# One decoder layer in float32: the down-projection as seven block products with their sums held in PSUM, and banded attention scores on 128 rows

## The chip, the cores and the metric

The kernel runs on one core of a Trainium2 chip. The metric is device time in microseconds, from the first to the last instruction with what the launch adds around them; a lower time is better. TensorE (PE, with its weight loads PEld) multiplies, VectorE (DVE), ScalarE (ACT) and GpSimd (POOL) do elementwise work, and SyncE (SP) issues the DMAs.

## The reference, cut to what matters

One layer of a decoder over 1024 tokens of width 1024, all in float32: a token mixer (attention over a window of 128 and a gated linear recurrence), cross-attention to 256 memory tokens, and a gated MLP of width 2816 with a convolution over three positions.

```python
s = einsum('bnqhgd,bnkhd->bnhgqk', q, [k_prev, k_here]) * 64**-0.5   # blocks of 128, heads of 64
u = h @ w_up                            # [1024, 2816*2]
u = causal_depthwise_conv3(u) + conv_b
gate, val = split(u, 2)
y = (gelu_tanh(gate) * val) @ w_down    # [1024, 2816] @ [2816, 1024]
x = x + rms_norm(y, ffn_post_norm)
```

## The kernel before, in words

Every product is made of three matmuls, since each operand x is split into a rounded part hi and a rest lo (`split`: a cast on ACT at L73, a subtraction at L74 on DVE or POOL): hi·hi, hi·lo and lo·hi. [...] The program is written in Python loops over tiles of 128 tokens or 128 features; a scheduler puts the instructions of each engine into one fixed order and inserts the waits. Buffers come from pools: `up` (U, 44 tiles of 4 KB per partition), `hs` (HS, 3), `hh` (HH, 3), and in PSUM `pj` (PJ, two tiles of two banks) and `sm` (SM, four tiles of one bank). A new tile takes the place of an older one, and its first writer waits for the last user of that one, whichever engine or DMA that is. SP issues all DMAs, in order.

*Attention scores* (`swa`, a generator that is advanced by `tick` between other matmuls). A query tile `q[h]` holds, for head h, the hi part in the 64 partitions of that head and the lo part in the other 64; the key tile `kah[h]` holds the hi part of the keys in both halves. One matmul over 128 rows (L387) therefore gives hi·hi + lo·hi; a second one (L389) gives hi·lo over the 64 rows of the head alone, from one tile `kal` that holds both heads.

*Up-projection* (`Pair`, `prod`, L934). It is done as seven block products for each of 22 feature blocks j: 12 matmuls each, 84 per block. Their weight sums are made on DVE (`wprep`), and `up_load(j + 2)` loads the weights two blocks ahead. `gate` and `value` apply the convolution; `value` stores the 128x1024 result into `gd[j]` in DRAM.

*Down-projection* (`down`, `dn_prep`, L1122). The 22 row blocks of `w_dn` are taken in chunks of 2 and then five times 4. For each chunk, each of 8 token tiles and each half of 512 output columns, 3 matmuls per row block are summed in one SM tile, and DVE adds that into `yacc` (L1129). Per row block `gd[j]` and `w_dn` (512 KB each) are loaded and split. In the last chunk `finish` normalizes a tile, adds the residual `x2` and stores.

Of the kernel before, what the change touches and what calls it, by code (L numbers as in the profile page):

```python
# [18 lines left out]
P = 128  # L19
# [16 lines left out]
def tile_layer(ctx: ExitStack, tc: tile.TileContext, a: dict, out: bass.AP):  # L36
# [305 lines left out]
    swam = cpool.tile([P, 2 * P], F32, name="swam")  # L342
# [4 lines left out]
    late(dve.tensor_copy(lvm, lvf))  # L347
    AT = U("AT", (P, NB, P))
    late(pool.memset(AT, 0.0))
    Ad = cpool.tile([P, NB, 32], F32, name="Ad")  # L350
    late(pool.memset(Ad, 0.0))


    HEADS = (slice(0, 64), slice(64, P))

    def head_split(src, s):
        hi, lo = [U(s + "s", (P, 1024), F32R) for _ in range(2)], U(s + "l", (P, 1024), F32R)
        for h, r in enumerate(HEADS):
            act.copy(hi[h][r], src[r])
            dve.tensor_tensor(lo[r], src[r], hi[h][r].bitcast(F32), op=ALU.subtract)  # L360
        return hi, lo

    kah, kal = head_split(ka, "ka")
    for h, r in enumerate(HEADS):
        sp.dma_start(kah[h][HEADS[1 - h]].bitcast(F32), kah[h][r].bitcast(F32))

    def q_split(src):
        hi, lo = head_split(src, "qa")
# [6 lines left out]
    def swa(j, q):  # L375
        for g in range(2):
            s = [HS("s", (P, 2, 2, 2 * P)) for _ in range(2)]
            mx = ST("mx", 8)
            for i in range(2):
                pss = [SM("s", (P, 2, 2 * P)) for _ in range(2)]  # L380
                first = g == 0 and i == 0
                for b in range(2):
                    n = g * 4 + 2 * i + b
                    lo = P if n == 0 else 0
                    qc, kc = slice(n * P, (n + 1) * P), slice((n - 1) * P + lo, (n + 1) * P)
                    for h in range(2):
                        pe.matmul(pss[h][:, b, lo:], q[h][:, qc], kah[h][:, kc], start=True, stop=False)  # L387
                    for h, r in enumerate(HEADS):
# [433 lines left out]
    gd = dram.tile([NF, P, T], F32, name="gd")  # L822

    hR = []

# [133 lines left out]
    def value(u, j, g):  # L959
        c = HH("c")  # L960
        conv(u, NF + j, c)
        dve.tensor_tensor(c, g, c, op=ALU.mult)
        sp.dma_start(gd[j], c)

    class Pair:
        def __init__(self, j, x=None, z=None):
# [92 lines left out]
    up_load(3)  # L1059
    for j in range(2, NF):  # L1060
        prev, cur = cur, Pair(j)
        cur.q1()
        wprep(j, 3)
        wprep(j, 7)
        cur.q5()
        wprep(j + 1, 1)
        wprep(j, 4)
        up_load(j + 2)
        cur.q2()
        wprep(j + 1, 5)  # L1070
        wprep(j + 1, 2)
        cur.q6()
# [9 lines left out]
    w_fpost = bcast_row(a["ffn_post_norm"], "wfp", U)  # L1082
    chunks = [(0, 1)] + [tuple(range(c, c + 4)) for c in range(2, NF, 4)]
    dn = {}

    def dn_prep(j):
        g, w = HS("g"), HH("wd")
        sp.dma_start(w, w_dn[j * P:(j + 1) * P, :])
        sp.dma_start(g, gd[j])
        dn[j] = split_u(g, "g"), split_u(w, "wd")  # L1090

    yacc = [None] * NB

    def finish(tb, yw, ss, xt):
# [3 lines left out]
        for ch in range(2):  # L1098
            c = slice(ch * 512, (ch + 1) * 512)
# [3 lines left out]
    def down(n, js):  # L1103
        last, fin = n == len(chunks) - 1, None
        junk = U("junk") if last else None
        nxt = [] if last else list(chunks[n + 1])
        for tb in range(NB):
            if yacc[tb] is None:
                yacc[tb] = U("yacc")
            if last:  # L1110
                xt, yw, ss = HH("x2"), HS("yw"), ST("ss", 2)
                sp.dma_start(xt, x2d[tb])
            if tb % 2 == 1 and nxt:
                dn_prep(nxt.pop(0))
            for ch in range(2):
                c = slice(ch * 512, (ch + 1) * 512)
                ps = SM("dn")
                m = 0
                for j in js:
                    (ghi, glo), (whi, wlo) = dn[j]  # L1120
                    for l, r in ((ghi, whi), (ghi, wlo), (glo, whi)):
                        pe.matmul(ps, l[:, tb * P:(tb + 1) * P], r[:, c],  # L1122
                                  start=(m == 0), stop=(m == 3 * len(js) - 1))
                        m += 1
                y = yacc[tb][:, c]
                if n == 0:
                    act.copy(y, ps)
                else:
                    dve.tensor_tensor(y, ps, y, op=ALU.add)  # L1129
                if last:  # L1130
                    act.activation(junk[:, c], y, AF.Square, scale=1.0 / 32, accum_out=ss[:, ch:ch + 1])  # L1131
                    dve.tensor_tensor(yw[:, c], y, w_fpost[:, c], op=ALU.mult)
            if last:
                if fin is not None:
                    finish(*fin)
                fin = (tb, yw, ss, xt)
            yield
        if last:
            finish(*fin)
        for j in js:  # L1140
            dn[j] = None
# [58 lines left out]
```

## Time and profile before

| what | value |
|---|---|
| median of 3 runs | 1460.9 us (1457.65 to 1462.75) |
| the profiled execution, its time | 1458.89 us |
| its span, first to last instruction | 1457.1 us |
| granted clock of TensorE, mean | 0.996 |
| PE busy | 1428.9 us (98%) |
| DVE busy | 877.3 us (60%) |
| ACT busy | 623.5 us (43%) |
| POOL busy | 82.0 us (6%) |
| DMA | 130.69 MB, mean 90 GB/s |

Busy is the time in which an engine had an instruction in work. A matmul's stated length includes the time in which it overlaps its neighbours, so how fast matmuls follow each other is read from their starts. POOL issues no DMA in this kernel.

### The profile page before, as it was taken

How to read it: one execution, taken by the hardware profiler on the slowest of the kernel's cores; microseconds unless marked ns; L12 is line 12 of the kernel's file. 1: busy time of each engine (PE TensorE's matmuls, PEld its weight loads, DVE VectorE, ACT ScalarE, POOL GpSimd, SP SyncE). 2: the span in 40 equal slices, each digit the busy share in tenths (PEclk: the TensorE clock that was granted, in tenths of full speed). 3: DMA queues.
4: the chain of work that ended last, by engine and by line, in shares of the span. 5: the costliest groups of instructions: out<-in, count | busy, mean ns of one | idle time of the engine just before them, and what ended most of it. 6: DMA issues, size and time to landing. Idle time of an engine off the chain costs nothing.

```text
span 1457.1 us, 21512 instructions
## 1 busy us (share of the span) xinstructions
PE 1428.9 (98%) x8770; PEld 1183.8 (81%) x8770; DVE 877.3 (60%) x1263; ACT 623.5 (43%) x1156; POOL 82.0 (6%) x148
## 2 busy tenths in 40 slices
PE   7999999999999999999999999999999999999997
PEld 6978887777898888887888788888888877888886
DVE  4446616565675553457347997787777747444436
ACT  4453533526454433345335655555454537212102
POOL 3100100000010110011111000000000000000001
PEclk9999999999999999999999999999999999999999
DMA  7132102020853252013223332222222127333104
GB/s 225 37 94 45 30 8 52 16 60 20 213 152 106 91 174 58 1 44 130 87 87 101 84 104 87 70 76 87 88 87 82 48 72 270 120 116 116 59 29 159
DMA packets 121872, 130.69 MB, mean 90 GB/s; under 512 B 12789, under 2 KB 100270, under 8 KB 121774
## 3 DMA queue, kind: packets, MB, share of 16 engines
q1 hardware_dynamic: 121774, 129.32, 28.6%
q8 instruction: 69, 1.13, 0.3%
q14 instruction: 29, 0.24, 0.0%
HBM read 101.52 MB, written 25.17 MB: 87 GB/s over the span
## 4 chain that ended last, share of the span: by engine, by line
PE 91%; DVE 5%; ACT 2%; DMA 1%; issue 1%; POOL 0%; SPq 0%; DVEq 0%; POOLq 0%; ACTq 0%
PE xz L934 22%; PE dn L1122 16%; PE co L676 6%; PE po L676 6%; PE cq L236 5%; PE y L934 4%; PE pv L256 3%; PE pqa L236 3%; PE pm L649 3%; PE pf L236 3%; PE pg L236 3%; PE pq L236 3%; PE cq L227 2%; PE sc L764 1%; PE po L444 1%; PE lv L459 1%
## 5 line engine op out<-in xcount | busy, mean ns | idle before, releaser
L934 PE MATMUL xz<-th,w 128*128 128x512 f32 x960 | 306.5, 393 | 2.3 <-DVE ug L994 1.2
L934 PEld LDWEIGHTS xz<-th,w 128*128 128x128 f32 x960 | 180.2, 188 | 48.6 <-DVE ug L994 5.9
L934 PE MATMUL xz<-tl,w 128*128 128x512 f32 x480 | 187.1, 390 | 0.0
L1122 PE MATMUL dn<-wdl,gh 128*128 128x512 f32 x352 | 137.1, 389 | 0.1
L1122 PE MATMUL dn<-wdh,gh 128*128 128x512 f32 x352 | 136.2, 390 | 0.8 <-ACT wdh L73 0.8
L1122 PE MATMUL dn<-wdh,gl 128*128 128x512 f32 x352 | 137.0, 389 | 0.0
L1129 DVE TENSOR_TENSOR yacc<-dn,yacc 128x512 f32<-128x512 f32 x80 | 55.1, 690 | 96.5 <-PE dn L1122 95.8
L934 PEld LDWEIGHTS xz<-tl,w 128*128 128x128 f32 x480 | 90.2, 188 | 17.4
L74 DVE TENSOR_TENSOR wl<-w,wh 128x1024 fp32r<-128x1024 f32 x59 | 73.1, 1249 | 32.1 <-ACT wh L73 32.0
L73 ACT CAST w<-w 128x512 fp32r<-128x512 f32 x105 | 62.6, 621 | 43.8 <-PE xz L934 30.2
L74 DVE TENSOR_TENSOR w<-w,w 128x512 fp32r<-128x512 f32 x105 | 69.9, 688 | 18.2 <-ACT w L73 17.9
L1122 PEld LDWEIGHTS dn<-wdh,gh 128*128 128x128 f32 x352 | 66.0, 188 | 15.1 <-ACT wdh L73 1.2
L1122 PEld LDWEIGHTS dn<-wdl,gh 128*128 128x128 f32 x352 | 66.1, 188 | 14.3 <-DVE wdl L74 0.5
L1122 PEld LDWEIGHTS dn<-wdh,gl 128*128 128x128 f32 x352 | 66.1, 188 | 13.8
L73 ACT CAST wh<-w 128x1024 fp32r<-128x1024 f32 x64 | 66.0, 1056 | 10.4 <-DMA w<-in_ca_wq 5.1
L73 ACT CAST gh<-g 128x1024 fp32r<-128x1024 f32 x22 | 23.1, 1052 | 101.4 <-PE dn L1122 91.8
L934 PE MATMUL y<-th,w 128*128 128x512 f32 x168 | 55.2, 389 | 0.0
L883 DVE TENSOR_TENSOR s<-w 128x512 f32<-128x512 f32 x21 | 14.5, 691 | 50.8 <-PE xz L934 50.8
L1131 ACT ACTIVATE junk<-yacc 128x512 f32<-128x512 f32 x16 | 10.1, 633 | 73.4 <-DVE yacc L1129 73.4
L398 DVE SCALAR_TENSOR_TENSOR s<-s,swam 128x512 f32<-128x512 f32 (+2 forms) x40 | 20.7, 553 | 33.3 <-PE s L389 33.3
L676 PE MATMUL po<-wh,mh 128*128 128x512 f32 x128 | 40.0, 393 | 0.0
L676 PE MATMUL co<-VWh,pth 128*128 128x512 f32 x128 | 40.0, 393 | 0.0
(310 smaller groups left out, 3260.9 us busy)
## 6 DMA issues: line engine op xcount, KB each, us to landing
w<-in_ffn_w_up SPq DMA_DIRECT2D x44, 512.0 KB, 4.7
gd<-c SPq DMA_DIRECT2D x22, 512.0 KB, 2.6
g<-gd SPq DMA_DIRECT2D x22, 512.0 KB, 5.7
wd<-in_ffn_w_down SPq DMA_DIRECT2D x22, 512.0 KB, 3.4
x<-in_x SPq DMA_DIRECT2D x16, 512.0 KB, 3.1
w<-in_w_in SPq DMA_DIRECT2D x16, 512.0 KB, 7.2
w<-in_ca_wk SPq DMA_DIRECT2D x8, 512.0 KB, 5.7
w<-in_ca_wv SPq DMA_DIRECT2D x8, 512.0 KB, 5.5
```

The lines of the kernel that those rows point to most:

```text
L73: act.copy(hi, src)
L74: eng.tensor_tensor(lo, src, hi.bitcast(F32), op=ALU.subtract)
L227: pe.matmul(ps[:, t0:t0 + n], l[:, k, :], r[:, k % 2, c:c + n], start=(m == 0), stop=(m == 23))
L236: pe.matmul(ps[:, half * 512:(half + 1) * 512], l[:, k, :], hts[half][k // 2][sel][:, k % 2, :], start=(k == 0 and j == 0), stop=(k == KD ...
L256: pe.matmul(ps[:, tb % 4, :], l[:, k % 2, c:c + P], r[:, k % 4, :], start=(m == 0), stop=(m == 23))
L398: dve.scalar_tensor_tensor(s[i][:, b0:b1, h, lo:], pss[h][:, b0:b1, lo:], 0.125, swam[:, lo:].rearrange("p (a k) -> p a k", a=1) .to_broad ...
L444: pe.matmul(po[r, b, :], va[:, n - 1 + kb, r], ptt[:, h, kb, :], start=(kb == kbs[0]), stop=(kb == 1))
L649: pe.matmul(ps[:, i, :], l[:, k, :], r[:, k % 4, :], start=(n == 0), stop=(n == 23))
L676: pe.matmul(ps[:, ch * 512:(ch + 1) * 512], l, r[:, ch * 512:(ch + 1) * 512], start=(k == 0 and j == 0), stop=(k == KD - 1 and j == 2))
L934: pe.matmul(ps, l[k], r[k // 2][:, k % 2, :], start=start and m == 0, stop=stop and m == last, skip_group_check=True)
L1122: pe.matmul(ps, l[:, tb * P:(tb + 1) * P], r[:, c], start=(m == 0), stop=(m == 3 * len(js) - 1))
L1129: dve.tensor_tensor(y, ps, y, op=ALU.add)
```

## The change

Three parts. **Down-projection:** tokens, features and output columns are each cut in two, and the product of 2x2 blocks is made of seven block products (`PASSES`, the numbers of the up-projection's products). One pass goes over 11 pairs of row blocks (m) and four token tiles (b): 12 matmuls per step, 77 steps. Its four results stay in PSUM from pass to pass (`bank_a` in the four SM tiles, `bank_b` in the two PJ tiles) and are drained after a pass. The left operands (tokens by features) are summed on DVE in `rows_out`, after `value`, and stored as eight half-size pieces of `gd`. The right operands (sums of blocks of `w_dn`) are made by DMAs that POOL issues (`dn_sums`): into a tile `ws` with plain and adding DMAs, and from there into `wsd` in DRAM. Each step loads two pieces of 256 KB (`dn_load`), ahead by 5 to 16 steps, and splits them (`dn_ahead`). **Scores:** the keys' lo part gets a tile per head that holds it in both halves, so the second matmul runs over 128 rows as well (and adds lo·lo). **Buffers:** `hh` has 4 tiles; `swam` and `Ad` move into one of them.

```diff
-    hh = ctx.enter_context(tc.tile_pool(name="hh", bufs=3))
+    hh = ctx.enter_context(tc.tile_pool(name="hh", bufs=4))
...
+    kal = [U("kal", (P, 1024), F32R) for _ in range(2)]
+    kah = head_split(ka, "ka", kal)
+    for t in (kah, kal):
+        for h, r in enumerate(HEADS):
+            sp.dma_start(t[h][HEADS[1 - h]].bitcast(F32), t[h][r].bitcast(F32))
...
                         pe.matmul(pss[h][:, b, lo:], q[h][:, qc], kah[h][:, kc], start=True, stop=False)
-                    for h, r in enumerate(HEADS):
-                        pe.matmul(pss[h][:, b, lo:], q[h][r, qc], kal[r, kc], start=False, stop=True)
+                        pe.matmul(pss[h][:, b, lo:], q[h][:, qc], kal[h][:, kc], start=False, stop=True)
...
-        sp.dma_start(gd[j], c)
+        rows_out(j, c)
+    def rows_out(j, c):
+        m = j // 2
+        if j % 2 == 0:
+            t = U("gt", (P, 2, 512))
+            dve.tensor_tensor(t[:, 0], c[:, :512], c[:, 512:], op=ALU.subtract)
+            sp.dma_start(gd[1, m], c[:, :512])
+            sp.dma_start(gd[5, m], t[:, 0])
+            held[m] = c, t
+        else:
+            c0, t = held.pop(m)
+            t4 = U("gt", (P, 512))
+            dve.scalar_tensor_tensor(t[:, 1], t[:, 0], -1.0, c[:, 512:], op0=ALU.mult, op1=ALU.subtract)
+            dve.tensor_tensor(c0[:, 512:], c[:, 512:], c0[:, 512:], op=ALU.subtract)
+            dve.scalar_tensor_tensor(t4, t[:, 1], -1.0, c[:, :512], op0=ALU.mult, op1=ALU.subtract)
...
+    def dn_sums(m):
+        t = U("ws", (P, 2, 512))
+        pool.dma_start(t[:, 0], dn_src(0, 1, m))
+        pool.dma_start(t[:, 1], dn_src(0, 0, m))
+        pool.dma_start(t[:, 0], dn_src(1, 1, m), accum_op=ALU.add)
+        pool.dma_start(t[:, 1], dn_src(0, 1, m), accum_op=ALU.add)
+        pool.dma_start(wsd[5, m], t[:, 0])
+        pool.dma_start(wsd[7, m], t[:, 1])
+        pool.dma_start(t[:, 0], dn_src(0, 0, m), accum_op=ALU.add)
+        pool.dma_start(wsd[6, m], t[:, 0])
+        pool.dma_start(t[:, 0], dn_src(1, 0, m), accum_op=ALU.add)
+        pool.dma_start(wsd[3, m], t[:, 0])
+    PASSES = (1, 5, 6, 3, 7, 2, 4)
+    steps = [(n, m) for n in PASSES for m in range(NM2)]
...
+    def dn_mm(ps, i, b, start, stop):
+        hi, lo = dn_op[i]
+        c = slice(b * P, b * P + P)
+        for k, (l, r) in enumerate(((hi, hi), (hi, lo), (lo, hi))):
+            pe.matmul(ps, l[:, 0, c], r[:, 1, :], start=start and k == 0, stop=stop and k == 2,
+                      skip_group_check=True)
...
+            for m in range(NM2):
+                i = p * NM2 + m
+                more = max(0, min(11, (i - 3 * NM2) // 2))
+                dn_ahead(i, *((7, 4) if p == 0 else (5 + more, 2 + more)))
+                for b in range(4):
+                    dn_mm(bank[b], i, b, n in (1, 5, 2) and m == 0, m == NM2 - 1)
...
     cur.q3()
-    next(first)
+    go(1)
     cur.q7()
     g = gate(cur.ug, NF - 1)
-    next(first)
+    go(2)
     cur.q4()
```

On PE the scores of one block pair of the first head pair (`s` the PSUM tiles, `kas` and `kal` the keys, `qas` the queries) stand before as follows.

```order
L387 MATMUL s_805<-kas_692,qas_758 128x256
L387 MATMUL s_806<-kas_693,qas_759 128x256
L389 MATMUL s_805<-kal_694,qas_758 128x256
L389 MATMUL s_806<-kal_694,qas_759 128x256
L387 MATMUL s_805<-kas_692,qas_758 128x256
L387 MATMUL s_806<-kas_693,qas_759 128x256
L389 MATMUL s_805<-kal_694,qas_758 128x256
L389 MATMUL s_806<-kal_694,qas_759 128x256
```

Now a head has its two matmuls next to each other, and all read 128 rows; the number of matmuls is the same.

On POOL, behind the norms of the cross-attention, the first of eleven sums (pair m = 0) stands now; the names in brackets are semaphores of the DMAs that a row waits for (DMASW: those that POOL issued, in turn 0 to 7).

```order
L1001 DMA ws_7704<-in_ffn_w_down 128x512 [waits DMAHW0_49,DVE_49,PE_49]
L1002 DMA ws_7704<-in_ffn_w_down 128x512
L1003 DMA ws_7704<-in_ffn_w_down 128x512 [waits DMASW0_49]
L1004 DMA ws_7704<-in_ffn_w_down 128x512 [waits DMASW1_49]
L1005 DMA wsd<-ws_7704 128x512 [waits DMASW2_49]
L1006 DMA wsd<-ws_7704 128x512 [waits DMASW3_49]
L1007 DMA ws_7704<-in_ffn_w_down 128x512 [waits DMASW4_49]
L1008 DMA wsd<-ws_7704 128x512 [waits DMASW6_49]
L1009 DMA ws_7704<-in_ffn_w_down 128x512 [waits DMASW7_49]
L1010 DMA wsd<-ws_7704 128x512 [waits DMASW0_49]
```

Nothing stood there before. L1001, L1003, L1005, L1007, L1008, L1009 and L1010 each wait for the one before: seven links. On SP, in the up-projection, the load of block 7's weights (`w_8194`, `w_8195`) stands among the stores of the pieces of blocks 3 and 4.

```order
L992 DMA gd<-gt_8111 128x512 [waits DMAHW0_49,DVE_49]
L879 DMA w_8194<-in_ffn_w_up 128x8x128 [waits DMASW5_49,DMASW7_49,DMASW3_49,DMAHW1_49,DMASW2_49,Activation_49]
L879 DMA w_8195<-in_ffn_w_up 128x8x128 [waits DMAHW2_49,PE_49,Activation_49]
L979 DMA gd<-c_8250 128x512 [waits DMAHW3_49,DVE_49]
L980 DMA gd<-gt_8255 128x512 [waits DMAHW4_49,DVE_49]
```

The load takes the place of the tile `ws` of m = 1 and so waits for the end of that sum; the loads of blocks 9, 11, ... 19 do the same for m = 2, 3, ... 8. Before, no load of weights waited for POOL's DMAs, as there were none, and one store per block stood there.

## Rows read from the trace of the kernel before

**Rows 1.** The page: busy time by engine, and the chain by engine.
```profile
PE 1428.9 (98%) x8770; PEld 1183.8 (81%) x8770; DVE 877.3 (60%) x1263; ACT 623.5 (43%) x1156; POOL 82.0 (6%) x148
...
PE 91%; DVE 5%; ACT 2%; DMA 1%; issue 1%; POOL 0%; SPq 0%; DVEq 0%; POOLq 0%; ACTq 0%
```
**Rows 2.** Stretches: length, busy PE PEld DVE ACT POOL, clock, DMA share, GB/s.
```profile
57.00:385.00 328.00, 326.38 (x3019) 262.33 (x3019) 168.84 (x301) 145.37 (x320) 18.82 (x31) 0.99 0.21 55
...
1214.00:1450.00 236.00, 235.65 (x1039) 194.40 (x1037) 123.04 (x152) 59.05 (x87) 6.02 (x14) 1.00 0.35 121
```
**Rows 3.** Stretches: one block of the up-projection, columns as in rows 2.
```profile
1038.40:1057.63 19.23, 19.23 (x86) 15.61 (x85) 14.69 (x20) 9.85 (x15) 0.00 (x0) 1.00 0.27 83
```
**Rows 4.** The chain in order of time: start, us, what.
```profile
437.02 8.64 PE pm L649 x72
...
1213.28 236.38 PE dn L1122 x1040
```
**Rows 5.** Timeline of PE, score matmuls: start, us of the piece, what, how many.
```profile
75.67 0.22 PE L387 MATMUL s<-kas,qas 128*128 128x128 f32 x1
...
76.08 0.38 PE L387 MATMUL s<-kas,qas 128*128 128x256 f32 x1
76.39 0.38 PE L389 MATMUL s<-kal,qas 64*128 64x256 f32 x1
76.70 0.73 PE L236 MATMUL pg<-hTl,wh 128*128 128x512 f32 x2
...
78.77 0.50 PE L387 MATMUL s<-kas,qas 128*128 128x256 f32 x2
79.20 0.38 PE L389 MATMUL s<-kal,qas 64*128 64x256 f32 x2
79.52 0.50 PE L387 MATMUL s<-kas,qas 128*128 128x256 f32 x2
...
344.17 0.38 PE L389 MATMUL s<-kal,qas 64*128 64x256 f32 x1
```
**Rows 6.** Waits of PE from 57 to 385 us: total, times, longest.
```profile
PE tt L245 <- ACT vtmp L610: 1.1, 1, 1.1
PE ot L538 <- DVE on L529: 0.2, 1, 0.2
```
**Rows 7.** Timeline of DVE in one block of the up-projection.
```profile
1043.88 0.69 DVE L883 TENSOR_TENSOR s<-w 128x512 f32<-128x512 f32 x1 [3.46 <-PE xz L934]
```
**Rows 8.** DMA issues: count, KB each, median us from issue to landing.
```profile
w<-in_ffn_w_up SPq DMA_DIRECT2D x44, 512.0 KB, 4.7
...
out<-yw SPq DMA_DIRECT2D x16, 256.0 KB, 2.1
...
w<-in_w_out SPq DMA_DIRECT2D x8, 256.0 KB, 4.7
```
**Rows 9.** Timelines of POOL and DVE at two places.
```profile
23.34 0.31 POOL L391 MEMSET s<- 128x256 f32 x1
...
23.43 1.28 DVE L114 SCALAR_TENSOR_TENSOR x<-x,rstd,wmix 128x1024 f32<-128x1024 f32 x1 [0.77 <-POOL rstd L84]
...
659.15 2.41 POOL L74 TENSOR_TENSOR wl<-w,wh 128x1024 fp32r<-128x1024 f32 x1 [2.18 <-ACT wh L73]
...
659.81 2.83 DVE L74 TENSOR_TENSOR wl<-w,wh 128x1024 fp32r<-128x1024 f32 x1
```
**Rows 10.** The page's groups: busy, mean ns of one, idle before.
```profile
L74 DVE TENSOR_TENSOR wl<-w,wh 128x1024 fp32r<-128x1024 f32 x59 | 73.1, 1249 | 32.1 <-ACT wh L73 32.0
...
L73 ACT CAST gh<-g 128x1024 fp32r<-128x1024 f32 x22 | 23.1, 1052 | 101.4 <-PE dn L1122 91.8
```
**Rows 11.** Timeline of PE between the two projections, rows with idle time.
```profile
1201.62 0.50 PE L934 MATMUL xz<-th,w 128*128 128x512 f32 x1 [1.16 <-DVE ug L994]
...
1205.46 0.50 PE L934 MATMUL xz<-th,w 128*128 128x512 f32 x1 [0.78 <-DVE uv L998]
...
1212.02 1.19 PE L1122 MATMUL dn<-wdh,gh 128*128 128x512 f32 x4 [0.77 <-ACT wdh L73]
```
**Rows 12.** The chain after the last matmul.
```profile
1449.69 0.70 DVE yacc L1129
```

More of the change, by code (lines that the diff above doesn't have):

```diff
@@ L821, in tile_layer @@
     x2d = dram.tile([NB, P, D], F32, name="x2d")
-    gd = dram.tile([NF, P, T], F32, name="gd")
+    gd = dram.tile([8, NF // 2, P, 512], F32, name="gd")
+    wsd = dram.tile([8, NF // 2, P, 512], F32, name="wsd")
     hR = []
@@ L1002, in q4, with dn_load, dn_ahead @@
             act.copy(self.uv[:, :512], self.x)
+    NM2 = NF // 2
+    PASSES = (1, 5, 6, 3, 7, 2, 4)
+    steps = [(n, m) for n in PASSES for m in range(NM2)]
+    dn_raw, dn_op = [], []
+    def dn_load():
+        n, m = steps[len(dn_raw)]
+        t = U("dn", (P, 2, 512))
+        sp.dma_start(t[:, 1], {1: dn_src(0, 0, m), 2: dn_src(1, 0, m), 4: dn_src(1, 1, m)}.get(n, wsd[n, m]))
+        sp.dma_start(t[:, 0], gd[n, m])
+        dn_raw.append(t)
+    def dn_ahead(i, la, sa):
+        while len(dn_raw) < min(i + la, len(steps)):
+            dn_load()
+        while len(dn_op) < min(i + sa, len(steps)):
+            k = len(dn_op)
+            dn_op.append(split_u(dn_raw[k], "dn", (P, 2, 512)))
+            dn_raw[k] = None
     pend = None
@@ L1079, in tile_layer, with fin_half, finish @@
             g = gate(cur.ug, j)
[L1082 to L1090, printed above, removed]
-    yacc = [None] * NB
-    def finish(tb, yw, ss, xt):
+    def dn_mm(ps, i, b, start, stop):
[4 more added lines that the diff above has]
+                      skip_group_check=True)
+    bank_a, bank_b = [], []
+    yacc = [None] * NB
+    n1, n2 = slice(0, 512), slice(512, 1024)
+    fins = {}
+    def fin_half(tb, src, ch):
+        if tb not in fins:
+            fins[tb] = HH("x2"), HS("yw"), ST("ss", 2)
+            sp.dma_start(fins[tb][0], x2d[tb])
+        xt, yw, ss = fins[tb]
+        c = (n1, n2)[ch]
+        act.activation(junk[:, c], src, AF.Square, scale=1.0 / 32, accum_out=ss[:, ch:ch + 1])
+        dve.tensor_tensor(yw[:, c], src, w_fpost[:, c], op=ALU.mult)
+    def finish(tb):
+        xt, yw, ss = fins.pop(tb)
         r = ST("rstd", 1)
@@ L1097, in finish @@
         pool.tensor_tensor(r, r, mhalf[:, :1], op=ALU.pow)
-        for ch in range(2):
-            c = slice(ch * 512, (ch + 1) * 512)
+        for c in (n1, n2):
             dve.scalar_tensor_tensor(yw[:, c], yw[:, c], r[:, 0:1], xt[:, c], op0=ALU.mult, op1=ALU.add)
             sp.dma_start(out[tb * P:(tb + 1) * P, c], yw[:, c])
[L1103 to L1136, printed above, removed]
-            yield
[L1138 to L1141, printed above, removed]
@@ L1143, in tile_layer, with drain_pass @@
-    for j in chunks[0]:
-        dn_prep(j)
-    first = down(0, chunks[0])
+    def drain_pass(n, b, ps):
+        tb = b if n in (1, 2, 4) else b + 4
+        if n == 1 or n == 5:
+            yacc[tb] = yacc[tb] or U("yacc")
+            act.copy(yacc[tb][:, n1 if n == 1 else n2], ps)
+        elif n == 6:
+            act.copy(yacc[tb][:, n1], ps)
+        elif n != 4:
+            y = yacc[tb][:, n2 if n == 7 else n1]
+            dve.tensor_tensor(y, ps, y, op=ALU.add)
+        if n == 4:
+            fin_half(tb, ps, 1)
+            finish(tb)
@@ new lines, in tile_layer, with down @@
+    later = []
+    def down():
+        for p, n in enumerate(PASSES[:-1]):
+            if n == 1:
+                bank_a.extend(SM("dn") for _ in range(4))
+            elif n == 5:
+                for _ in range(2):
+                    t = PJ("dn", (P, 2, 512))
+                    bank_b.extend((t[:, 0], t[:, 1]))
+            elif n == 2:
+                for i in range(2):
+                    t = PJ("dn", (P, 2, 512))
+                    bank_b[2 * i:2 * i + 2] = [t[:, 0], t[:, 1]]
+            bank = (bank_a, bank_b)[p % 2]
+            for m in range(NM2):
[4 more added lines that the diff above has]
+                    dn_mm(bank[b], i, b, n in (1, 5, 2) and m == 0, m == NM2 - 1)
+                dn_op[i] = None
+                if later and m % 2 == 1:
+                    later.pop(0)()
+                yield
+            for b in range(4):
+                drain_pass(n, b, bank[b])
+            if n == 7:
+                for tb in range(4, NB):
+                    later.append(lambda tb=tb: (fin_half(tb, yacc[tb][:, n1], 0),
+                                                fin_half(tb, yacc[tb][:, n2], 1), finish(tb)))
+        base = 6 * NM2
+        for b in range(4):
+            fin_half(b, yacc[b][:, n1], 0)
+            for m in range(NM2):
+                dn_ahead(base + m, NM2, NM2)
+                dn_mm(bank_a[b], base + m, b, False, m == NM2 - 1)
+                if b == 3:
+                    dn_op[base + m] = None
+            drain_pass(4, b, bank_a[b])
+            yield
@@ L1146, in tile_layer, with go @@
+    steps_of = down()
+    def go(n):
+        for _ in range(n):
+            next(steps_of, None)
     cur.q3()
-    next(first)
+    go(1)
     cur.q7()
     g = gate(cur.ug, NF - 1)
-    next(first)
+    go(2)
     cur.q4()
-    next(first)
+    go(1)
     value(cur.uv, NF - 1, g)
-    for _ in first:
-        pass
-    for n, js in list(enumerate(chunks))[1:]:
-        for _ in down(n, js):
-            pass
+    w_fpost = bcast_row(a["ffn_post_norm"], "wfp", U)
+    dve.tensor_scalar(w_fpost[:, n2], w_fpost[:, n2], -1.0, None, op0=ALU.mult)
@@ L1161 @@
+    junk = U("junk")
+    for _ in steps_of:
+        pass
 _INS = ['x', 'mem', 'mix_pre_norm', 'w_in', 'attn_sinks', 'hgrn_lb_logits', 'hgrn_out_norm',
```

38 lines of the change are left out of this document (27 added, 11 removed).

## The prediction

> **What bounds the kernel now.** I read the page first: PE is busy 1428.9 us, 98% of a span of 1457.1 us, and the chain that ended last is PE for 91% and DVE for 5% [rows 1]. That is an average over stages, so I then cut out the stretches that the change touches. In the attention (57 to 385 us) PE is busy 326.38 of 328 us, DVE 168.84, ACT 145.37 [rows 2], and PE's waits there come to 1.3 us in two waits [rows 6]. One block of the up-projection takes 19.23 us, all of it PE, with DVE at 14.69 and ACT at 9.85 [rows 3]. In the down-projection PE is busy 235.65 of 236 us and moves 121 GB/s at a DMA share of 0.35 [rows 2]. So in all three PE ends last: a matmul taken away is worth what it occupies there, and other work costs nothing until it no longer fits beside PE. The question is how much room each stage has.
>
> **Down-projection, matmuls.** Before: 8 tiles x 2 halves x 22 row blocks x 3 = 1056 matmuls. The chain shows 1040 of them in one piece of 236.38 us [rows 4], so 236.38 / 1040 = 0.2273 us each. After: 77 steps x 12 = 924, of the same shape, 132 fewer. 132 x 0.2273 = **-30.0 us**.
>
> **Down-projection, feed.** A step is 12 x 0.2273 = 2.73 us and loads two pieces of 256 KB, 524,288 bytes: 192 GB/s. The trace moves 121 GB/s at a share of 0.35 [rows 2], which makes about 346 GB/s at a full share (estimate), so 0.56 of the DMA engines. While the look-ahead grows (from the fourth pass on, one and a half steps are loaded per step), 288 GB/s, a share of 0.83. The splits take 1.05 us of ACT and 1.25 of DVE per step [rows 10], 1.58 and 1.88 at the higher rate, under 2.73 with the drains beside them. It fits, but tightly. Below: nothing is lost. Above: the growth happens over 22 steps, and if DMA gave only two thirds of the 288 GB/s, 11 extra steps at 2.73 us would be late by half, 15 us. I take **+2** (0 to +15), nearer to the lower end since PE of before is busy in all but 0.35 us of this stage [rows 2], that is, waits for no transfer.
>
> **Scores.** There are 128 score matmuls. From the start of each to the start of the next matmul on PE, over all 128 (the first at 75.67 us, the last at 344.17), they take 30.2 us, 0.236 each. [rows 5] show how: where a matmul over 128 rows and one over 64 alternate, each takes 0.31 (76.08, 76.39, 76.70). Two over 128 rows in succession take 0.43 (78.77 to 79.20): the second starts about 0.12 behind the first, since the piece of two is 0.50 long and one alone 0.38. Two over 64 rows run side by side (the piece of two is 0.38, as one alone), but take 0.32 to the next start. So what costs is the change between the shapes. A matmul of 256 columns with no such change takes 8.64 / 72 = 0.120 us [rows 4]. After, all read 128 rows: 128 x 0.120 = 15.4, **-14.8** at most. At the other end the switch is not what costs and nothing is gained (0). I take **-13**, near the first end because the nearest rows are these matmuls themselves, a little less because some of the freed time goes to places where PE waits for DVE or ACT [rows 6]. The added work (two more copies of the keys' lo part by SP, once per head pair's keys, and none on DVE) lies before the first score and beside PE's projections.
>
> [...]
>
> **Up-projection, DVE.** `rows_out` adds one 128x512 operation in even blocks and three in odd ones, at 0.69 us each [rows 7]: 4 x 0.69 = 2.76 per pair of blocks. 2 x 14.69 + 2.76 = 32.1 of 38.46 us [rows 3]. DVE waits for PE there (3.46 us ahead of the row in [rows 7]), and 6.3 us per pair are left: **0**.
>
> **Up-projection, POOL's sums.** Ten DMAs per pair, seven links in series. Who waits: the load of a later block's weights on SP, which takes the place of `ws`, and behind it in SP's queue the stores of the pieces; behind that, PE. By the order of the instructions and the block time of [rows 3], the load is issued about 33 us after the sum starts and its weights are needed about 12 us later still, but each pair needs the chain done within its 38.46 us, or the delay accumulates. The trace has no DMA of POOL and no adding one. The nearest rows are DMAs of 256 KB on SP's queue: 2.1 us for a store, 4.7 for a load [rows 8]. Seven links: 14.7 to 32.9 us, both below 38.46: **0**. Every us beyond it comes 11 times. At the end two sums follow each other, but the down-projection needs their first result only some 30 us later (its second pass).
>
> [...]
>
> **Boundaries.** Between the projections PE idles 1.16, 0.78 and 0.77 us [rows 11], waiting for DVE's `ug` and `uv` and ACT's `wdh`. Now 12 or 24 down matmuls lie between the products there, 2.7 us or more of PE's work per wait: **-2.7** (-3 to 0). At the end the last tile no longer passes through the addition into `yacc` of 0.70 us [rows 12]: **-0.7**. At the start of the MLP, where DVE sets the pace, one operation of 0.69 more (block 0's `rows_out`) [rows 7]: **+0.6**.
>
> **Sum.** The profiled execution took 1458.89 us, 1457.1 of it span, 1.8 around it. 1458.9 - 30.0 - 13 - 2.7 - 0.7 + 0.6 + 2 = 1415.1. The median of the runs is 2.0 above the profiled execution: **1417**.
>
> **The rivals.**
>
> *B, POOL's sums hold the up-projection (the other side).* Place: SP's load of blocks 7, 9, ... 19. Nothing else in the program works in this way, and seven links by one engine's issue may each be slower than any row here. If a link takes more than 38.46 / 7 = 5.5 us, 11 pairs each lose 7 x the excess. The gains of the rest are 43.8 us, 4.0 per pair; so it decides from 42.4 us per chain, 6.1 per link. If a link that reads and writes memory takes the load and the store of [rows 8] together, 6.8 us, the chain is 47.6 and 11 x 9.1 = +100, about 1517 us. [...] Against: the longest row of 256 KB is 4.7, and DMA is at a share of 0.27 there [rows 3].
>
> *C, POOL and DVE hinder each other.* A DVE subtraction ran 2.83 us beside a POOL operation with two inputs (659.15 to 661.56), while its group's mean is 1.249; beside a POOL memset a DVE operation ran 1.28 [rows 9, 10]. If POOL's work on a DMA held DVE for about 1 us, less than the 1.58 that this row lost, 10 of them per pair are 10 us where DVE has 6.3: +3.7 x 11 = +41, about 1458, no change. It begins at 0.63 us per DMA. [...]
>
> [...]
>
> *D, the down-projection is fed too slowly.* The shares above are from loads of 512 KB in rows of 4 KB; each piece is now 128 rows of 2 KB, and a 256 KB load of before took as long as a 512 KB one, 4.7 us [rows 8]. Gaps of PE ahead of the down matmuls, +10 to +25: 1427 to 1442.
>
> *E, the scores gain nothing,* because what shows as the cost of a change of shape is something else, or because two 64-row matmuls that ran side by side now follow each other: -13 becomes 0, or, with 32 such pairs losing 0.120 us each [rows 4], +3.8. 1430 to 1434. Against: the 0.31 of a single 128-row matmul ahead of a 64-row one, in which nothing ran side by side [rows 5].
>
> **How the numbers follow.** A measurement of this kernel can tell about 0.3%, 4.4 us, from no change. Main case: 0.62, 1408 to 1426 by its own bounds (-1.8 and -2 from the scores and the feed; a slower feed above). D 0.13, E 0.07, C 0.05, B 0.13. Faster: main, D, E, and of B the 0.02 in which the chain lies between 38.5 and 42 us, and about 0.01 of C: 0.85. Same: 0.02 of C. Slower: the rest of B (0.11) and 0.02 of C: 0.13. The range of 8 in 10 takes in the main case, E and D: 1406 to 1445; what it leaves out is B, C and a little at the lower end.
>
> **What would show it.** Right: 924 down matmuls starting 0.227 us apart with no gap from pass to pass; score matmuls 0.12 apart with no step at the second of a head; blocks of the up-projection still 19.2 us, with DVE busy about 16 of it; POOL's DMAs landing within 5.5 us each. B would show as PE waiting at `prod` for weights, SP's queue at the load waiting for POOL's DMAs, and blocks in pairs above 38.5 us. C would show as DVE rows above 0.69 and 1.25 us beside POOL's issues. D would show as PE idle ahead of down matmuls, released by ACT's or DVE's split with a DMA behind it. E would show as score rows still some 0.24 apart. Most likely to make the forecast wrong is a link of POOL's sums longer than any row here.

## The result, and the profile after

The change made the kernel faster: 1418.83 us median of 4 runs (1416.69 to 1420.67) against 1461.47 (1457.65 to 1462.75), a ratio of 0.9712 with a 95% interval of 0.9688 to 0.9736. A second set of runs of the same kernel gave 1418.97 us and 0.9716 (0.9699 to 0.9733). 1417 us was forecast. The profiled execution after took 1420.67 us, 1418.5 of it span; the one before, from which the sum was made, 1458.89 and 1457.1. So the two traces to be compared differ by 38.2 us, where the sum had 43.8.

The page of after: busy time by engine, the chain by engine, and three groups of DMA issues (count, KB each, median us to landing).

```profile
PE 1385.2 (98%) x8638; PEld 1157.0 (82%) x8638; DVE 893.1 (63%) x1273; ACT 649.7 (46%) x1185; POOL 164.7 (12%) x258
...
PE 92%; DVE 3%; ACT 2%; DMA 1%; issue 1%; POOL 1%; SPq 1%; DVEq 0%; POOLq 0%; ACTq 0%
...
w<-in_ffn_w_up SPq DMA_DIRECT2D x44, 512.0 KB, 5.7
...
ws<-in_ffn_w_down POOLq DMA_DIRECT2D x66, 256.0 KB, 4.3
...
wsd<-ws POOLq DMA_DIRECT2D x44, 256.0 KB, 2.7
```

PE is still the bound, and it has 132 matmuls fewer, as the change says. The weights' loads by SP take a little longer than in [rows 8] (5.7 for 4.7 us).

Where the 38.2 us are shows in the chains of both traces, cut at the same four places. The place names are those of PE's long pieces: the end of the cross-attention (`co`), the first and the last up-projection piece of 60 matmuls, and the last down matmul.

| stretch | before, us | after, us | difference, us | forecast, us |
|---|---|---|---|---|
| to the end of `co` | 777.2 | 761.6 | -15.6 | -13 |
| to the first piece of 60 | 68.9 | 73.6 | +4.8 | +0.6 |
| to the last piece of 60 | 327.1 | 326.4 | -0.7 | 0 |
| to the last down matmul | 276.5 | 248.4 | -28.2 | -30.7 |
| to the last store's issue | 4.0 | 3.3 | -0.7 | -0.7 |
| to the end, with what lies around the span | 5.2 | 7.4 | +2.2 | 0 |

The forecast of -30.7 is the sum of three terms (-30.0 for the matmuls, +2 for the feed, -2.7 for the boundary waits).

The timeline of PE in the scores of the first head pair, after (start, us, what):

```profile
77.40 0.28 PE L392 MATMUL s<-kas,qas 128*128 128x256 f32 x1
77.52 0.28 PE L393 MATMUL s<-kal,qas 128*128 128x256 f32 x1
77.64 0.28 PE L392 MATMUL s<-kas,qas 128*128 128x256 f32 x1
77.75 0.28 PE L393 MATMUL s<-kal,qas 128*128 128x256 f32 x1
```

They start 0.12 us apart, where single ones in [rows 5] took 0.31. Summed from start to start over all 128 they take 17.0 us, 30.2 before: -13.2. So 2.4 us of the attention's -15.6 are something else. The windows of before show it (length, busy PE PEld DVE ACT POOL, granted clock, DMA share, GB/s):

```profile
168.00:172.00 4.00, 4.00 (x21) 3.89 (x21) 2.16 (x4) 0.00 (x0) 0.00 (x0) 0.57 0.44 131
...
267.00:271.00 4.00, 4.00 (x17) 3.44 (x17) 2.11 (x3) 0.00 (x0) 0.00 (x0) 0.57 0.45 133
```

Twice PE ran at a granted clock of 0.50 for 3.4 us (168.2 to 171.6 and 267.2 to 270.6), without having been idle (busy 7.98 of the 8 us ahead of the first, 6.98 of the 7 ahead of the second); that is some 1.7 us lost each time (an estimate, 3.4 x 0.50), 3.4 together, a us more than the 2.4. After, the clock is 1.00 in the whole stretch from 57 to 385 us.

The waits of PE after, over the whole span (total, times, longest), and the windows at the two that are new:

```profile
PE dn L1165 <- DVE dnl L74: 2.7, 1, 2.7
PE z L939 <- DVE w L74: 2.4, 1, 2.4
...
PE z L939 <- ACT w L73: 1.2, 1, 1.2
```
```profile
795.00:800.00 5.00, 1.72 (x7) 0.78 (x5) 4.86 (x5) 3.98 (x7) 0.00 (x0) 0.86 0.04 17
800.00:805.00 5.00, 4.72 (x11) 3.80 (x12) 4.35 (x7) 2.47 (x4) 0.00 (x0) 0.50 0.70 225
...
1217.00:1219.00 2.00, 0.00 (x0) 0.00 (x0) 1.56 (x3) 0.00 (x0) 0.00 (x0) 0.85 1.04 392
...
1221.00:1225.00 4.00, 4.00 (x11) 3.17 (x10) 3.59 (x4) 2.53 (x3) 0.00 (x0) 0.50 1.05 387
```

Behind each of the two idle stretches (1.2 + 2.4 us at the start of the MLP, 2.7 us in the down-projection) PE is busy again but at 0.50: 11 matmuls in 4 us, where 18 fit at 0.227 us each. So a wait of 2.7 us cost nearly six in this execution. What made the second one is in the timeline of DVE (in square brackets: idle time before, and what ended it) and in the chain:

```profile
1210.20 1.22 DVE L74 TENSOR_TENSOR dnl<-dn,dnh 128x1024 fp32r<-128x1024 f32 x1
1217.44 0.43 DVE L1262 TENSOR_SCALAR wfp<-wfp 128x512 f32<-128x512 f32 x1 [6.02 <-DMA wfp<-in_ffn_post_norm]
1217.78 4.91 DVE L74 TENSOR_TENSOR dnl<-dn,dnh 128x1024 fp32r<-128x1024 f32 x4
```
```profile
1211.46 5.96 DMA wfp<-in_ffn_post_norm
...
1219.06 190.92 PE dn L1165 x827
```

The change has one line that multiplies the final norm's weights `w_fpost` by -1 on DVE, in code right behind their load, and that load stands in SP's queue behind the last stores of `rows_out`. DVE waits 6.0 us at this line for the load, with two finished casts lying behind it (ACT ended them by 1207.3 us, DVE subtracts from 1217.78), and PE runs out of split operands.

The second set of runs of the same kernel has a trace too. There the wait is 1.7 us, the clock does not fall behind it, and the same 827 matmuls take 2.9 us less:

```profile
1219.35 188.03 PE dn L1165 x827
```

The stretch to the last down matmul is 244.5 us there, 32.0 less than before, where the forecast had 30.7 less.

The first wait shows in the timeline of ACT, after and then before:

```profile
796.02 0.59 ACT L1037 COPY ug<-x 128x512 f32<-128x512 f32 x1 [1.02 <-PE x L939]
796.50 0.62 ACT L73 CAST w<-w 128x512 fp32r<-128x512 f32 x1
```
```profile
809.63 1.21 ACT L947 ACTIVATE c<-uv,par 128x1024 f32<-128x1024 f32 x1
810.73 1.65 ACT L73 CAST w<-w 128x512 fp32r<-128x512 f32 x3
812.28 0.59 ACT L990 COPY ug<-x 128x512 f32<-128x512 f32 x1
```

The cast of block 1's weights for product 3 (`z` in the waits) stood ahead of the copy that waits for PE's product 6; now it stands behind it, and DVE's part of the same split stands behind all of block 0's `value`.

The up-projection is as forecast. Two blocks, windows as above:

```profile
1046.33:1065.53 19.20, 19.20 (x85) 15.62 (x85) 15.19 (x21) 8.64 (x13) 1.43 (x2) 1.00 0.52 154
1065.53:1084.73 19.20, 19.20 (x85) 15.62 (x85) 16.28 (x23) 10.61 (x16) 5.45 (x8) 1.00 0.75 194
```

PE is busy throughout, DVE at 31.5 of 38.4 us (32.1 was forecast). One chain of POOL's sums in the timeline of POOL:

```profile
1027.38 0.55 POOL L1001 DMA_DIRECT2D ws<-in_ffn_w_down  x1 [11.12 <-PE y L939]
...
1030.54 0.89 POOL L1003 DMA_DIRECT2D ws<-in_ffn_w_down  x1 [2.05 <-DMA ws<-in_ffn_w_down]
...
1048.47 0.87 POOL L1009 DMA_DIRECT2D ws<-in_ffn_w_down  x1 [6.06 <-DMA wsd<-ws]
1052.95 0.56 POOL L1010 DMA_DIRECT2D wsd<-ws  x1 [3.60 <-DMA ws<-in_ffn_w_down]
```

From the first issue to the last store's landing at 1055.24 us it takes 27.9 us. The eight chains that a later block's weights wait for take 28.9 us in the mean (27.9 to 29.7), 4.1 per link, and 9.5 less than two blocks.

### The profile page after: what moved, and what is told of

Its sections match the earlier page's. It is cut to its first block, busy times and chain, and to the rows that moved or that the text cites. A ratio compares the mean times of both kernels' runs of the same rounds, so it can differ in the third digit from the quotient of the medians.

```text
span 1418.5 us, 21778 instructions
## 1 busy us (share of the span) xinstructions
PE 1385.2 (98%) x8638; PEld 1157.0 (82%) x8638; DVE 893.1 (63%) x1273; ACT 649.7 (46%) x1185; POOL 164.7 (12%) x258
## 4 chain that ended last, share of the span: by engine, by line
PE 92%; DVE 3%; ACT 2%; DMA 1%; issue 1%; POOL 1%; SPq 1%; DVEq 0%; POOLq 0%; ACTq 0%
PE xz L939 23%; PE dn L1165 14%; PE co L680 6%; PE po L680 6%; PE cq L236 5%; PE y L939 4%; PE pqa L236 3%; PE pm L653 3%; PE pf L236 3%; PE pv L256 3%; PE pq L236 3%; PE pg L236 3%; PE cq L227 2%; PE sc L768 1%; PE po L448 1%; PE lv L463 1%
## 5 line engine op out<-in xcount | busy, mean ns | idle before, releaser
L74 DVE TENSOR_TENSOR dnl<-dn,dnh 128x1024 fp32r<-128x1024 f32 x77 | 90.5, 1219 | 56.0 <-ACT dnh L73 53.6
L1165 PE MATMUL dn<-dnl,dnh 128*128 128x512 f32 x308 | 121.3, 394 | 2.7 <-DVE dnl L74 2.7
L1165 PE MATMUL dn<-dnh,dnl 128*128 128x512 f32 x308 | 121.0, 393 | 0.0
L1165 PE MATMUL dn<-dnh 128*128 128x512 f32 x308 | 120.0, 392 | 0.0
L73 ACT CAST dnh<-dn 128x1024 fp32r<-128x1024 f32 x77 | 76.8, 1053 | 48.9 <-PE dn L1165 21.1
L74 DVE TENSOR_TENSOR wl<-w,wh 128x1024 fp32r<-128x1024 f32 x59 | 73.1, 1250 | 29.8 <-ACT wh L73 29.7
L1165 PEld LDWEIGHTS dn<-dnl,dnh 128*128 128x128 f32 x308 | 58.5, 190 | 15.8 <-DVE dnl L74 3.5
L1165 PEld LDWEIGHTS dn<-dnh,dnl 128*128 128x128 f32 x308 | 58.6, 190 | 12.2
L1165 PEld LDWEIGHTS dn<-dnh 128*128 128x128 f32 x308 | 58.5, 190 | 12.1
L953 DVE SCALAR_TENSOR_TENSOR c<-uv,par,c 128x1023 f32<-128x1023 f32 x22 | 28.2, 1284 | 63.8 <-ACT c L952 63.8
L952 ACT ACTIVATE c<-ug,par 128x1024 f32<-128x1024 f32 x22 | 27.4, 1245 | 41.3 <-DVE ug L1041 41.1
```

Source lines behind the costliest of these rows:

```text
L73: act.copy(hi, src)
L74: eng.tensor_tensor(lo, src, hi.bitcast(F32), op=ALU.subtract)
L952: act.activation(c, u, AF.Identity, scale=conv_w(2, j), bias=conv_b(j))
L953: dve.scalar_tensor_tensor(c[:, 1:], u[:, :T - 1], conv_w(1, j), c[:, 1:], op0=ALU.mult, op1=ALU.add)
L1165: pe.matmul(ps, l[:, 0, c], r[:, 1, :], start=start and k == 0, stop=stop and k == 2, skip_group_check=True)
```

## The experiments

**1. The scores alone**, in the kernel before:

```diff
-                    for h, r in enumerate(HEADS):
-                        pe.matmul(pss[h][:, b, lo:], q[h][r, qc], kal[r, kc], start=False, stop=True)
+                        pe.matmul(pss[h][:, b, lo:], q[h][:, qc], kal[h][:, kc], start=False, stop=True)
```

(with `kal` as a tile per head in both halves, as in the change).

> The kernel before with the 128-row scores alone. My theory: what costs is the change between 128-row and 64-row matmuls, so the 128 score matmuls go from 30.2 to about 17 us (-13), and the two stretches at a granted clock of about 0.5 that the trace of before shows around 168 and 268 us, right behind such alternating matmuls, go away too (-3): about 1445 us. Rival 1: the scores give -13 but the two stretches stay: about 1448 us. Rival 2: the gain comes only together with the rest of the change (buffers, order): 1455 to 1461 us.

Measured: 1445.61 us, ratio 0.9905 (0.9887 to 0.9924). The 128 matmuls take 16.9 us from start to start. The windows of this run:

```profile
168.00:172.00 4.00, 4.00 (x26) 3.48 (x26) 2.85 (x7) 3.53 (x23) 1.34 (x2) 1.00 0.35 97
...
267.00:271.00 4.00, 4.00 (x26) 3.11 (x25) 3.09 (x5) 2.90 (x14) 3.14 (x4) 1.00 0.01 2
```

The -13 and the full clock are both there without the rest of the change.

**2. The same with the order of before**: both heads' first matmuls, then both heads' second ones.

```diff
+                    for h in range(2):
                         pe.matmul(pss[h][:, b, lo:], q[h][:, qc], kal[h][:, kc], start=False, stop=True)
```

> The kernel before with 128-row scores, but in the order of before (both heads' first matmuls, then both heads' second ones). My theory: the rows' number is what counts, so 128 matmuls take about 17 us from start to start, and one run gives 1443 to 1447 us. Rival: the order by head, two matmuls into one PSUM tile in succession, is what made them fast: 25 us or more, 1453 us or more.

Measured: 1445.78 us in the one run; the matmuls take 17.0 us. So it is the rows, not the order by head: a matmul at a change between 128 and 64 rows takes 0.31 us to the next start in [rows 5], and one of this run, which has no such change, takes 0.12 (77.82 to 77.94). Why it takes longer at a change, no row shows.

**3. The change without the scores**: the changed kernel with `kal` and the second matmul as before (the diff of experiment 1 reversed).

> The changed kernel with the scores as before (64-row matmuls for the keys' lo part). My theory, by the sums from the traces: the scores and the two half-clock stretches beside them cost what they did before, so 16 us over the changed kernel: about 1434 us, and the two stretches at a granted clock of about 0.5 near 168 and 268 us are back. Rival: the parts do not add, because the wait at the start of the MLP or the down-projection hangs on the attention's end; then 1425 or 1445 us.

Measured: 1432.26 us, ratio 0.9813 (0.9795 to 0.9832). The parts add: 0.9813 x 0.9905 = 0.9720, and the whole change has 0.9712. But the two stretches at half clock were not there, though the 64-row matmuls were:

```profile
168.00:172.00 4.00, 4.00 (x36) 4.00 (x37) 3.85 (x9) 0.00 (x0) 0.00 (x0) 1.00 0.44 131
...
267.00:271.00 4.00, 4.00 (x30) 3.66 (x29) 2.88 (x8) 0.74 (x1) 0.00 (x0) 1.00 0.17 50
```

So that part of the expectation failed: the half-clock stretches of before's trace are no fixed consequence of the 64-row matmuls. They are not that one execution's alone either. The trace of experiment 6, whose attention is that of before, has one at the first place:

```profile
168.00:172.00 4.00, 4.00 (x15) 3.05 (x15) 2.88 (x5) 0.00 (x0) 0.00 (x0) 0.65 0.14 39
```

So of the three traces with 64-row scores two have such stretches while the scores run (75 to 345 us). With 128-row scores, after and experiment 1 have 1.00 in the mean from 57 to 385 us. That the 64-row matmuls make them likelier is not shown, and the 2.4 us are what they were worth in one execution.

**4. The norm's weights later**:

```diff
     value(cur.uv, NF - 1, g)
+    go(20)
     w_fpost = bcast_row(a["ffn_post_norm"], "wfp", U)
```

> The changed kernel with the load of the final norm's weights and the DVE multiplication by -1 behind it issued 20 steps later in the down-projection. My theory: at 1211 to 1217 us DVE waits 6.0 us for that load, and the splits behind it leave PE idle for 2.7 us and, after that, at a granted clock of 0.5 for some 6 us (2.9 us lost): about -5.5 us, 1413 us, and no idle of PE in the down-projection. Rival: the loads of gd behind SP's queue are late as well, at 1219 us, so PE waits for ACT's casts instead: 0 to -2.5 us.

Measured: 1413.16 us, ratio 0.9682 (0.9664 to 0.9700). Its chain has one piece for nearly the whole stage:

```profile
1203.42 201.60 PE dn L1165 x888
```

201.60 / 888 = 0.2270 us each: no gap and no stretch at half clock. The stretch to the last down matmul is 242.6 us (248.4 after). The wait was the load's, and the late loads of `gd` cost nothing.

**5. One tile from another pool**: block 0's `gt` taken from `hs`.

```diff
-            t = U("gt", (P, 2, 512))
+            t = (U if j else HS)("gt", (P, 2, 512))
```

> The changed kernel with the tile gt of block 0 alone taken from the pool hs in place of up; the subtraction into it stays. My theory of the 3.6 us idle of PE and the stretch at half clock behind it at the start of the MLP: the additional tile in the pool up makes every later tile there take the place of one that comes free later, so the weights' split for product 3 falls behind value of block 0. Then PE has under 1 us of idle there, the clock stays at 1.0, and the time falls by 5 to 6 us against the changed kernel (about 1413 us). Rival: the additional DVE operation itself (0.69 us) and the order of the code cost it; then the stretch stays as it is and the time is that of the changed kernel within 2 us.

Measured: 1417.38 us, ratio 0.9713 (0.9695 to 0.9730). The stretch from the end of `co` to the first piece of 60 took 71.1 us (73.6 after, 68.9 before), and product 3 no longer waits; instead

```profile
PE x L939 <- DVE uv L1045: 1.6, 1, 1.6
PE y L939 <- DVE w L74: 0.7, 1, 0.7
```

with the clock at 1.00. So the place of the tile did cause the wait for product 3, but the gain (2.6 us in the trace) is half of what I expected, and not to be told from none in the times.

**6. The tile alone, in the kernel before**:

```diff
         sp.dma_start(gd[j], c)
+        if j == 0:
+            t = U("gt", (P, 2, 512))
+            dve.tensor_tensor(t[:, 0], c[:, :512], c[:, 512:], op=ALU.subtract)
+            sp.dma_start(gd[0, :, :512], t[:, 0])
+            sp.dma_start(gd[0], c)
```

> The kernel before with one more tile taken from the pool up in value of block 0, with one more subtraction of 128x512 on DVE into it and its store (the store's place in gd is written over by gd's own). My theory: this one tile shifts which older tile each later one replaces, and block 1's splits fall behind value, as in the changed kernel: +3 to +6 us over the kernel before, with 2 us or more of idle of PE on product 3 of block 1. Rival: the wait belongs to the other edits there (the order of t3 and the weights): +0 to +1 us.

Measured: 1466.70 us, ratio 1.0048 (1.0027 to 1.0068), +5.9 us. PE waits at the same two places as in the changed kernel, and longer:

```profile
PE z L934 <- ACT w L73: 3.1, 1, 3.1
PE z L934 <- DVE w L74: 2.3, 1, 2.3
```

The other edits of the change are not in this kernel, so the wait does not need them. The operation is 0.69 us long and the stretch from the end of `co` to the first piece of 60 is 75.1 us, 6.2 over before. This run alone does not part the tile from its operation and its store; experiment 5 does, since it keeps the operation and takes only the tile away, and the wait for product 3 goes. So most of it is the order into which ACT and DVE fall when this tile is taken from the pool.

**7. The code's order at the start of the MLP**:

```diff
+    wprep(1, 3)
+    t3()
     value(uv, 0, g)
     cur.q6()
-    wprep(1, 3)
-    t3()
     wprep(1, 7)
```

> The changed kernel with the weights of product 3 and the sums t3 of block 1 prepared ahead of value of block 0 in the code; the pools stay as in the changed kernel. My theory (the wait at the start of the MLP is one of order on ACT and DVE): PE idles under 1 us there, the clock stays at 1.0, about 5 us less than the changed kernel, 1413 to 1415 us. Rival: value of block 0 is now late and the wait only moves to the next products (ug, uv of block 1): 0 to -2 us.

Measured: 1418.88 us, ratio 0.9719 (0.9702 to 0.9736): the rival. Product 3 has its weights in time, and the next product waits (`PE x` for DVE's `w`, 2.8 us).

**8. No sums**:

```diff
     def dn_sums(m):
+        return
...
-        sp.dma_start(t[:, 1], {...}.get(n, wsd[n, m]))
+        sp.dma_start(t[:, 1], {...}.get(n, dn_src(0, 1, m)))
```

> The changed kernel without POOL's weight sums: the ten DMAs per pair are left out, and the steps that would read a sum load the plain right half of a row block instead, so the down-projection adds up other products. My theory: the sums cost nothing, since a chain of theirs ends within the time of two blocks; the time stays that of the changed kernel within 2 us (1415 to 1420), and the blocks of the up-projection stay at 19.2 us. Rival: POOL's DMAs lengthen the loads that SP issues (5.7 us where the kernel before had 4.7) or DVE's operations, and the time falls by 4 us or more.

Measured: 1416.47 us, ratio 0.9699 (0.9684 to 0.9713), blocks of the up-projection with PE busy throughout as above. The intervals overlap with that of the changed kernel, and the medians differ by 2.4 us. In the traces none of it is in the up-projection (326.5 us from the first to the last piece of 60, 326.4 after); the span ends 3.3 us behind the last store's issue without the sums and 5.3 with them. The sums do not lengthen DVE's operations either. The page's group of 105 subtractions, after and then before (busy us, mean ns, idle before):

```profile
L74 DVE TENSOR_TENSOR w<-w,w 128x512 fp32r<-128x512 f32 x105 | 66.8, 683 | 0.4 <-ACT w L73 0.4
```
```profile
L74 DVE TENSOR_TENSOR w<-w,w 128x512 fp32r<-128x512 f32 x105 | 69.9, 688 | 18.2 <-ACT w L73 17.9
```

**9 and 10. Longer chains of sums**, by two and by five more adding DMAs:

```diff
+        for _ in range(5):
+            pool.dma_start(t[:, 0], dn_src(1, 0, m), accum_op=ALU.add)
         pool.dma_start(wsd[3, m], t[:, 0])
```

> The changed kernel with two more adding DMAs of 256 KB at the end of each chain of POOL's sums (so the fourth sum holds more than it should). A chain took about 29 us in the trace of the changed kernel; two more links at about 4.5 us make it 38, against 38.4 us for two blocks. My theory: at most 3 us more than the changed kernel. Rival: the load of weights that waits for the chain is already at its limit, and each added us costs eight to eleven times: +70 us or more.

> The changed kernel with five more adding DMAs at the end of each chain of POOL's sums (the fourth sum holds more than it should). My theory: a chain takes about 51 us, 13 over the 38.4 of two blocks; the loads of blocks 7 to 21 wait for the chains, less some 12 us of slack at first: +80 to +130 us, about 1500 to 1550 us, with PE waiting at prod for weights and SP at the load. Rival: the loads are far enough ahead that only the end is late: under +20 us.

Measured: with two, 1433.66 us, ratio 0.9826 (0.9790 to 0.9862); with five, 1536.20 us, ratio 1.0526 (1.0500 to 1.0552). The waits of PE in the up-projection, with two and with five:

```profile
PE xz L939 <- ACT ug L1039: 9.2, 7, 4.4
```
```profile
PE xz L939 <- ACT uv L1035: 99.8, 8, 22.9
```

With five, POOL issues the first DMA of the next chain as soon as the last of this one is out; two such rows of its timeline:

```profile
1017.70 0.57 POOL L1001 DMA_DIRECT2D ws<-in_ffn_w_down  x1
...
1069.82 0.57 POOL L1001 DMA_DIRECT2D ws<-in_ffn_w_down  x1
```

The first DMAs of the chains m = 1 to 8 are 52.4 us apart in the mean, 14.0 more than two blocks; eight times that is 112, and the stretch from the first to the last piece of 60 is 115.5 us longer than after (441.9 for 326.4). With two they are 39.1 apart, 0.7 more, and the stretch is 12.0 longer: 9.9 of it the waits of PE in that stretch, and 1.9 that 36 matmuls behind the longest of them took 10.06 us (0.279 each, from 885.98 us) where 0.2273 each makes 8.18. This misses my theory (at most 3): a chain from first issue to landing took 42.6 us, not 38. From two to five added links, 13.2 us more per chain cost 103.6 us, 7.8 for each.

What waits for the chains is not what the prediction named, SP's load, but ACT's cast of the weights, eight times; the load waits once. The waits of ACT and of SP, with five:

```profile
ACT w L73 <- DMA wsd<-ws: 116.8, 8, 25.2
```
```profile
SPq L879 <- DMA wsd<-ws: 8.5, 1, 8.5
```

Rival B of the prediction is thus a real limit, though not at the place that it named: some 9.5 us per chain away, and a us beyond it comes about eight times.

**11. Both waits taken away**: experiment 4, and block 0's `rows_out` behind the splits of block 1.

```diff
-    value(uv, 0, g)
+    c_first = value(uv, 0, g)
...
     t4()
+    rows_out(0, c_first)
     cur.q7()
```

> The changed kernel with both new waits of PE taken away: the norm's weights loaded 20 steps into the down-projection (as in wfp_late), and rows_out of block 0 called after t4 instead of inside value, so that its tile gt and its subtraction stand behind the splits of block 1's weights. My theory: 5 us less than the changed kernel from the first, and 2 to 5 from the second: 1408 to 1412 us, PE with under 1.5 us of idle at the start of the MLP. Rival: at the start of the MLP DVE sets the pace anyway, so the second gives nothing: 1413 us.

> The changed kernel unaltered, on the same chip as the run with both waits taken away, for the comparison: a ratio to the kernel before of 0.969 to 0.974, 1415 to 1421 us.

Measured: 1410.39 us (1408.51 to 1413.40), ratio 0.9658 (0.9638 to 0.9677); the changed kernel on the same chip 1418.97 (1418.08 to 1419.61). This is faster than the kernel before and the changed one. The stretch from the end of `co` to the first piece of 60 is 69.5 us, 0.6 over the 68.9 of before: the forecast's own term for the start of the MLP. PE's only wait there is the 1.6 us for DVE's `uv` that experiment 5 showed (I had expected under 1.5). What the second edit adds to experiment 4 (0.9682 to 0.9658) lies within the intervals; it is the trace that shows it, 69.5 us for 73.7.

## Why the prediction was right

**Down-projection, matmuls (-30.0).** Right: 924 at 0.227 us. **Feed (+2).** Too much: in experiment 4 no down matmul waits; the DMA share after, from 1250 to 1400 us, is 0.59, close to the 0.56 of the estimate. The stage's 2.5 us short of the forecast are not a slow feed (rival D) but the wait for the norm's weights, 2.7 us of idle and 190.92 - 827 x 0.2273 = 2.9 us at half clock. Against them stand the 2 us of the feed that were not needed and some 1 us more: without that wait (experiment 4) the stage is 33.9 us shorter than before, 1.2 more than 30.0 and the 2.7 of [rows 11]. I put that down to the matmuls right behind the old waits, where the next one started 0.34 us later (1201.62 to 1201.96, 1205.46 to 1205.80) and not 0.23; that this makes up the 1.2, no run shows by itself. The 2.9 us are that execution's: in the second trace of the same kernel the clock did not fall.

**Boundaries (-2.7).** Right that the waits of [rows 11] go, since down matmuls lie between the products; wrong that nothing takes their place. I had counted the DVE multiplication by its length and not by the load that it waits for, nor by what is queued behind it on DVE.

**Scores (-13).** Right in size (-13.2) and in cause (experiments 1 and 2); rival E fell. Two readings on the way were wrong. Of two 128-row matmuls in succession in [rows 5] the second starts 0.22 us behind the first (78.77 and 78.99), not 0.12: the first one behind a change is also the longer one, 0.39 us for 0.28. And rival E counted 32 pairs of 64-row matmuls side by side; the trace has 16. The sum used neither. The further 2.4 us of the profiled executions were clock, not scores.

**Start of the MLP (+0.6).** The step that failed: +4.8. The operation was costed right, as experiment 11 shows; what I left out is that its tile comes from the pool `up`, and that this moves block 1's splits behind `value` in the scheduler's order on two engines. I had the order of the changed program before me and read it only for the sums and the stores.

**POOL's sums (0), DVE in the up-projection (0).** Right: 28.9 us per chain inside the bounds of 14.7 to 32.9, and experiment 8 finds nothing in the up-projection. One sign of being right did not come: 14 of POOL's 110 DMAs took longer than 5.5 us to land, up to 7.0, and the chain was short enough all the same. The break-even was put at 42.4 us by counting eleven pairs. Eight wait, for the weights of blocks 7, 9, ... 21 (my list of the loads ended at 19), so chains 38.4 + 43.8 / 8 = 43.9 us apart would have taken all of the gain (an estimate; by the 12.0 us that experiment 9 lost at 39.1, somewhat less), and experiment 10 at 52.4 did end slower than before. Rival C fell: the 105 subtractions of the up-projection's weights took 683 ns in the mean on DVE, 688 before.

**Tail (-0.7).** Right. The span of after ends 5.3 us behind the last store's issue, 3.4 before (+1.9). It was 5.3 too without the scores and 3.3 without POOL's sums, but also 3.4 with the longest chains; what it hangs on stays open.

So the total is near 1417 because the big terms were right, and in part by luck. Against the sum, the start of the MLP is 4.2 us worse, the down-projection 2.5 and the end 2.2; the attention is 2.6 better, mostly by the clock, and the up-projection 0.7. Together +5.6: 1415.1 becomes the 1420.67 of the profiled execution, and the median of after is 1.8 below that. The forecast had put the median 2.0 above the profiled execution, as before the change. So a miss of 5.6 us between the traces became one of 1.8 between the forecast and the median, by where the profiled executions lay among the others.

## What to carry to other kernels

An instruction that waits for a DMA can hold up what is queued behind it on its engine: here 0.43 us of DVE work waited 6.0 us, and the splits behind it came late (1217.78 us, with two of their casts done by 1207.3). Place it where its data has long landed, however short it is. One more tile from a rotating pool can move a split that PE needs behind work that it does not; read the order of every engine at each place that takes a new tile, not only where the big edits are. And where a background chain has a fixed time per iteration, know its distance from the limit: here some 9.5 us of 38.4, with each us beyond it paid about eight times.

## What the hardware showed that I had not expected

The price of an idle stretch of PE was about twice its length where the granted clock fell to 0.50 behind it (2.7 us idle and 2.9 us lost at the norm's weights, after). It does not always fall. Five traces have PE idle for 2.6 to 2.7 us there. In after and experiment 7 the clock was 0.50 right behind it, and in experiment 9 the first 102 down matmuls behind it took 24.79 us, 0.243 each. In experiments 5 and 8 it did not fall: 1.00, and 188.06 us for 828 matmuls, 0.2271 each. In experiment 5 PE was idle for the same 2.7 us in the down-projection and ran at full clock right after it (idle to 1217.5 us, 1.00 in the window that follows it):

```profile
1215.00:1217.00 2.00, 0.00 (x0) 0.00 (x0) 1.09 (x2) 0.00 (x0) 0.00 (x0) 1.00 1.00 356
1217.00:1219.00 2.00, 1.48 (x6) 1.23 (x7) 1.91 (x3) 1.16 (x2) 0.00 (x0) 1.00 1.05 405
```

And it fell in the attention of before and of experiment 6 (0.57 and 0.65 over 4 us) with PE shown as busy throughout. The time of single runs follows it: of the kernel before, 1457.90 us at a mean granted clock of 0.998 and 1462.81 at 0.993, about 1 us per 0.001. That is as much as the smaller terms of a sum like this one, so a term of 3 us is read from the trace, or from several runs, and not from one time. Idle time of PE came just ahead of the stretches at 800 and 1219 us (3.6 and 2.7 us); what set off those at 168 and 267 us no run here shows.
